# Residual, norm and first projection: squares summed by matmuls, splits and tables made at other times

## The chip, the cores and the metric

The kernel runs on one core of a Trainium2 chip. The metric is the device time of one execution in microseconds (us), the median over several runs. The core's engines run side by side: TensorE (PE, the matmuls; PEld its weight loads), VectorE (DVE), ScalarE (ACT), GpSimd (POOL), and SyncE (SP), which here only issues DMAs. Each engine works through its own list of instructions in order and waits where an operand or a buffer is not ready.

## What is computed

Four layers on x, 512 tokens by 1024 features, in fp32. The first two come from one block, the last two from another. Cut to what matters here:

```python
def first_block(x, c, ...):
    for layer in range(2):
        mod = silu(c) @ w_ada[layer] + b_ada[layer]
        shift, scale, gate = mod[:, :D], mod[:, D:2 * D], mod[:, 2 * D:]
        h = _rms(x, norm_g[layer]) * (1 + scale) + shift
        if layer == 0:
            y = _gdn_mixer(h, ...)            # gated delta rule, ends in @ w_out_a
        else:
            mkv = silu(c) @ w_ada_kv + b_ada_kv
            hk = _rms(x, kv_norm_g) * (1 + mkv[:, D:]) + mkv[:, :D]
            kv = hk @ w_kv                    # keys and values of the attention
            y = _sb_mixer(h, k_sh, v_sh, ...) # stick-breaking attention, ends in @ w_out_b
        x = x + gate * y
    return x

def second_block(x, positions, ...):
    h = rmsnorm(x, norm1_gain)
    # window attention with rope on q and k, mLSTM, both from h @ w_in
    mixed = sigmoid(gate_a) * att_b + sigmoid(gate_m) * ml_b
    x = x + mixed @ w_out
    return x + peer_ffn(rmsnorm(x, norm2_gain), ...)

# rms: x * rsqrt(mean(x * x) + 1e-6) * gain
# stick-breaking: wts = exp(log_sigmoid(logits) + after), after = sum of
# log_sigmoid(-logits) over the keys between this one and the query
```

## The kernel before

Everything lies transposed: x is 8 blocks of 128 features (partitions) by 512 tokens. An fp32 product is three matmuls of a fast fp32 format (`mm3`, L122 to L124) on a high part H, a rounded copy made on ACT (L115), and a low part L, the difference, made on VectorE or POOL (L118). Weights come by DMA as `wr`, are split the same way into `wh` and `wl` by `wtile`, and their low parts go to POOL save for every ninth tile, which goes to VectorE.

**The stages** are gdn (layer 1), the stick-breaking attention (sb, layer 2), a second stage (window attention, mLSTM and `w_out`) and PEER. A scheduler of the framework orders each engine's instructions by a simulated time line. PSUM banks limit it: a projection takes its output bank from `pj`, two of them and now and then one that a stage leaves over.

**The end of a stage** is `residual`: output projection, block j of 8 added to x on VectorE (L346, or L344 without a gate), its square on ACT (L212), a running sum of the squares on VectorE (L214). Behind the last block `mean` sums that one tile over its partitions with `colsum`, four matmuls of 128x128 fp32 against a column of ones (L130), and `rsqrt` makes the reciprocal root: a scale on VectorE (L138), a power on POOL (L139). `rows_of` spreads the four columns by four transposes (L146). `modnorm` then makes each block of the normed x: with a shift a product on VectorE (L234), scale and shift on ACT (L235), the high part on ACT, the low part on VectorE for even blocks and POOL for odd ones; without a shift one instruction on VectorE (L232). The projections of the next stage follow.

A residual can run in parts of its k blocks, each added to x on its own, so that a part can run while later heads are still computed. gdn's takes 7 blocks and 1, sb's

```python
EARLY_A, EARLY_OUT = (slice(0, 7), slice(7, 8)), (slice(0, 6), slice(6, 8))
```

6 and 2; `w_out` has one part.

**sb** goes by 8 pairs of heads (`sb_pair`): logits (L838) with a mask (L841), three ACT operations on them (L846 to L848), a maximum and add on VectorE (L849), the split, the cumulative matmuls (L859), Exp on ACT (L862), the values (L868). Then the product with the gate (L815) and its split into oH and oL, block j of w_out_b's input. While one pair goes through its ACT chain, PE has other pairs' or projections' matmuls.

**The second stage** loads the window masks, the identity and the positions at its start, casts and copies the masks on VectorE (L1204 to L1207) and makes the rope tables from the positions by small VectorE instructions and two sines on ACT (L888 to L906, with a table load for the sine).

## Time and profile before

| what | value |
|---|---|
| median of 3 runs | 2786.94 us (2786.12 to 2788.62) |
| the profiled execution | 2788.73 us |
| its span, first to last instruction | 2786.9 us |
| mean granted clock of TensorE | 0.98 |
| PE busy | 2627.4 us, 94% |
| POOL busy | 1747.1 us, 63% |
| VectorE busy | 1691.1 us, 61% |
| ACT busy | 1207.9 us, 43% |

The three ends of stages lie at 512 to 525 us (gdn to sb), 876 to 901 (sb to the second stage) and 1483 to 1496 (second stage to PEER). In a timeline row the bracket tells how long the engine had been idle before the instruction and which instruction of which engine ended that; a row with xN is N equal instructions in a row, and its us is their whole time.

### The profile page before, as it was taken

The page shows a single profiled execution, that of the slowest core. Times are in us where ns is not written, and L with a number is a line of the kernel's source. Part 1 is how long each engine was busy: PE and PEld are TensorE (multiplying, and loading weights), DVE is VectorE, ACT ScalarE, POOL GpSimd, SP SyncE. Part 2 cuts the span into 40 slices and gives each one's busy share as a digit, 9 for nine tenths or more (in the row PEclk, how much of TensorE's full clock was granted, in tenths as well). Part 3 has the DMA queues.
Part 4 walks back from the last instruction along what each step waited for, and adds up shares of the span by engine and source line. Part 5 has one row for each costly group of instructions (what it writes and reads, how often), then busy time and mean ns, then how long its engine had stood idle before and what let it go on. Part 6 is the DMA issues. An engine that isn't in the chain of part 4 may idle for free. (4 is left out here: it accounts for less than half of the span.)

```text
span 2786.9 us, 40407 instructions
## 1 busy us (share of the span) xinstructions
PE 2627.4 (94%) x14601; PEld 2244.6 (81%) x14601; DVE 1691.1 (61%) x3080; ACT 1207.9 (43%) x2505; POOL 1747.1 (63%) x1350
## 2 busy tenths in 40 slices
PE   6999998799998899999998999999999999999998
PEld 4787777697776787887776889999999977777777
DVE  7767674624445565122232797797875177778886
ACT  5676663635664444233333333434434333333332
POOL 4899883544232533443464378878788478888876
PEclk9999999899998999999999999999999999999999
DMA  6343331222011111211222488888888889999996
GB/s 243 106 139 126 108 109 34 64 92 75 29 35 58 46 52 56 91 63 60 76 83 76 140 293 301 293 309 315 303 302 302 277 306 329 340 331 334 333 315 223
DMA packets 206793, 499.35 MB, mean 179 GB/s; under 512 B 18304, under 2 KB 106624, under 8 KB 203520
## 3 DMA queue, kind: packets, MB, share of 16 engines
q1 hardware_dynamic: 167856, 359.19, 38.2%
q0 software_dynamic: 36864, 134.23, 13.4%
q10 hardware_dynamic: 1872, 3.33, 0.4%
q8 instruction: 115, 1.88, 0.3%
q14 instruction: 86, 0.70, 0.1%
HBM read 444.26 MB, written 52.43 MB: 178 GB/s over the span
## 5 line engine op out<-in xcount | busy, mean ns | idle before, releaser
L118 POOL TENSOR_TENSOR wl<-wr,wh 128x256 fp32r<-128x256 f32 (+2 forms) x515 | 428.8, 852 | 470.6 <-ACT wh L115 431.2
L118 POOL TENSOR_TENSOR upl<-upr,uph 128x1024 fp32r<-128x1024 f32 x128 | 312.2, 2439 | 99.0 <-ACT uph L115 97.8
L115 ACT ACTIVATE wh<-wr 128x256 fp32r<-128x256 f32 (+2 forms) x556 | 228.7, 445 | 323.9 <-PE pj L123 118.4
L122 PE MATMUL pj<-nH,downh 128*128 128x384 f32 x1024 | 352.3, 344 | 2.4 <-ACT w L1567 1.3
L124 PE MATMUL pj<-nH,downl 128*128 128x384 f32 x1024 | 348.8, 341 | 1.8 <-DVE downl L118 1.8
L123 PE MATMUL pj<-nL,downh 128*128 128x384 f32 x1024 | 348.8, 341 | 0.0
L118 POOL TENSOR_TENSOR downl<-downr,downh 128x1024 fp32r<-128x1024 f32 x96 | 238.2, 2483 | 131.9 <-ACT downh L115 130.5
L1612 PE MATMUL acc<-uph,wwh 128*128 128x512 f32 x768 | 302.3, 399 | 9.2 <-ACT wwh L115 9.1
L1612 PE MATMUL acc<-upl,wwh 128*128 128x512 f32 x768 | 305.5, 398 | 0.0
L115 ACT ACTIVATE downh<-downr 128x1024 fp32r<-128x1024 f32 x128 | 135.4, 1059 | 307.8 <-PE pj L123 183.1
L118 DVE TENSOR_TENSOR wwl<-wo,wwh 128x384 fp32r<-128x384 f32 x128 | 205.0, 1603 | 59.1 <-ACT wwh L115 53.7
L1612 PE MATMUL acc<-uph,wwl 128*128 128x512 f32 x768 | 233.1, 399 | 5.5 <-DVE wwl L118 5.4
L122 PE MATMUL pj<-hH,wh 128*128 128x512 f32 x544 | 224.7, 413 | 2.4 <-ACT mo L1284 1.3
L124 PE MATMUL pj<-hH,wl 128*128 128x512 f32 x544 | 221.5, 408 | 0.9 <-POOL wl L118 0.8
L123 PE MATMUL pj<-hL,wh 128*128 128x512 f32 x544 | 215.8, 397 | 0.0
L115 ACT ACTIVATE uph<-upr 128x1024 fp32r<-128x1024 f32 x128 | 134.8, 1053 | 168.5 <-POOL upl L118 114.3
L122 PEld LDWEIGHTS pj<-nH,downh 128*128 128x128 f32 x1024 | 192.9, 188 | 5.4 <-ACT downh L115 1.6
L124 PEld LDWEIGHTS pj<-nH,downl 128*128 128x128 f32 x1024 | 192.9, 188 | 3.0 <-DVE downl L118 2.8
L123 PEld LDWEIGHTS pj<-nL,downh 128*128 128x128 f32 x1024 | 192.9, 188 | 0.3
L1612 PEld LDWEIGHTS acc<-uph,wwh 128*128 128x128 f32 x768 | 145.3, 189 | 48.3 <-ACT wwh L115 13.4
L1612 PEld LDWEIGHTS acc<-uph,wwl 128*128 128x128 f32 x768 | 145.1, 189 | 42.8 <-DVE wwl L118 7.7
L1612 PEld LDWEIGHTS acc<-upl,wwh 128*128 128x128 f32 x768 | 145.4, 189 | 34.9
(627 smaller groups left out, 6546.1 us busy)
## 6 DMA issues: line engine op xcount, KB each, us to landing
downr<-in_peer_down_j SPq DMA_DIRECT2D x128, 512.0 KB
upr<-in_peer_up_j SPq DMA_DIRECT2D x128, 512.0 KB
wr<-in_w_in SPq DMA_DIRECT2D x50, 512.0 KB
ada<-in_w_ada SPq DMA_DIRECT2D x48, 512.0 KB
wait<-w SPq DMA_DIRECT2D x128, 192.0 KB
wo<-wait SPq DMA_DIRECT2D x128, 192.0 KB
G<-stage SPq DMA_DIRECT2D x24, 1024.0 KB
Gt<-G SPq DMA_DIRECT2D x48, 512.0 KB
```

Source lines behind the costliest of these rows:

```text
L115: nc.scalar.activation(h, src, AF.Copy)
L118: return (eb or nc.vector).tensor_tensor(l, src, h.bitcast(F32), op=ALU.subtract)
L122: mm(out, lh, rh, start=start, stop=False)
L123: mm(out, lh, rl, start=False, stop=False)
L124: mm(out, ll, rh, start=False, stop=stop)
L1612: mm(po[z][b], lh[:, zs], rh[:, bs], start=False, stop=j == P - 1 and rh is uh and lh is l, skip_group_check=True)
```

## The change

1. `residual`: the running sum on VectorE is gone. Each block's square goes to a colsum of its own, all eight adding into one PSUM bank ("n", "l" and "q"), and `rsqrt` reads it.
2. w_out_b's parts are 7 blocks and 1.
3. `modnorm` with a shift, even blocks: product with scale and rows in one VectorE instruction, the high part on ACT with the shift as its bias, the low part on VectorE from the same; one ACT instruction less.
4. `wtile` puts the splits of the next weights behind the residual's last square (ACT) and the power (POOL); the splits of the second stage's gate weights stand behind the last normed block.
5. The rope tables are made in `setup`, the window masks in gdn; the identity is cast once. The ones are one column, set by a memset. What sb needs of constants is loaded at its start through a pool of its own.

```diff
-        self.ident, self.ones, sel = self.load_const(const, ("id", "one", "sel"))
+        self.ident, = self.load_const(const, ("id",))
+        self.ones = const.tile([P, 1], F32, name="ones")
+        nc.vector.memset(self.ones, 1.0)
...
+            sel, = self.load_const(tmp, ("sel",))
+            nc.vector.tensor_copy(self.selr, sel[:, :16])
+            self.tables(tmp)
...
+        eb = nc.gpsimd if k % 2 else nc.vector
+        late = late and eb is nc.vector
+        if shift is None or late:
             nc.vector.scalar_tensor_tensor(n, xT[:, k], scale[:, k:k + 1], r, op0=ALU.mult, op1=ALU.mult)
         else:
             nc.vector.tensor_tensor(n, xT[:, k], r, op=ALU.mult)
             nc.scalar.activation(n, n, AF.Identity, scale=scale[:, k:k + 1], bias=shift[:, k:k + 1])
-        self.split(H[:, k], L[:, k], n, eb=nc.gpsimd if k % 2 else nc.vector)
+        if late:
+            nc.scalar.activation(H[:, k], n, AF.Identity, bias=shift[:, k:k + 1])
+            ins = nc.vector.scalar_tensor_tensor(L[:, k], n, shift[:, k:k + 1], H[:, k].bitcast(F32), op0=ALU.add, op1=ALU.subtract)
+        else:
+            ins = self.split(H[:, k], L[:, k], n, eb=eb)
+        if eb is nc.vector:
+            self.normed = ins
...
+        ahead = [self.ahead.pop(0) for _ in range(2)] if self.ahead else []
...
-                for j, raw in enumerate(raws):
-                    self.split(wh[:, j, o], wl[:, j, o], raw[:, fs], eb=nc.gpsimd if self.uid % 9 else nc.vector)
+                with ExitStack() as st:
+                    for ins in ahead:
+                        st.enter_context(self.tc.issue_after(ins))
+                    for j, raw in enumerate(raws):
+                        self.split(wh[:, j, o], wl[:, j, o], raw[:, fs], eb=nc.gpsimd if self.uid % 9 else nc.vector)
...
             if last:
-                held["sq"] = self.square(out, src if scratch is None else scratch(j), held.get("sq"), nc.vector)
+                if j == 0:
+                    held["sums"] = self.pg(bank)
+                sq = src if scratch is None else scratch(j)
+                held["sq"] = nc.scalar.activation(sq, out, AF.Square)
+                self.colsum(held["sums"], sq, 1, j == 0, j == KC - 1)
...
-        self.rms = self.mean([held["sq"]], f"x{self.uid}")
+        self.rms = self.rsqrt(self.const, held["sums"][:, :NT], [NT], 1.0 / D, f"x{self.uid}")
+        self.ahead = [held["sq"].ins, self.power.ins] * 6
...
-    EARLY_A, EARLY_OUT = (slice(0, 7), slice(7, 8)), (slice(0, 6), slice(6, 8))
+    EARLY_A, EARLY_OUT = (slice(0, 7), slice(7, 8)), (slice(0, 7), slice(7, 8))
...
+            self.window_masks(rt)
...
-            idr, sbm, nui = self.load_const(kv, ("id", "sbm", "nui"), F32R)
...
-                idr, wp, wc = self.load_const(c1, ("id", "wp", "wc"), F32R)
...
-                cos, sin = self.rope_tables(c1)
+                idr, wmask, cos, sin = self.identr, self.wmask, self.cos, self.sin
...
+            self.psum(st, q=1)
+            self.residual(a["w_out"], (xH, xL), None, lambda j: x[:, j], x, "q", lambda j: mix[:, j])
```

The line numbers of the changed kernel are higher: L130, L138, L139, L146 and L118 stay, L346 is L367, L838 and L841 are L867 and L870, L859 is L888, L868 is L897.

**First place: PE behind pair 6's logits.** The last logits (`q_6`) and mask of pair 6, then w_out_b's matmuls (into `pj`, from oH and oL). Before; 41 more of these matmuls follow before the first L859 of pair 6:

```order
L838 MATMUL l_7879<-q_6_7787,kT 128x512
L841 MATMUL l_7879<-cr_sbm,cr_id 128x128
L122 MATMUL pj_8158<-oH_6144,wh_8177 128x512
L122 MATMUL pj_8190<-oH_6144,wh_8177 128x512
L123 MATMUL pj_8158<-oL_6145,wh_8177 128x512
L124 MATMUL pj_8158<-oH_6144,wl_8178 128x512
L123 MATMUL pj_8190<-oL_6145,wh_8177 128x512
L124 MATMUL pj_8190<-oH_6144,wl_8178 128x512
L122 MATMUL pj_8214<-oH_6144,wh_8215 128x512
L123 MATMUL pj_8214<-oL_6145,wh_8215 128x512
L124 MATMUL pj_8214<-oH_6144,wl_8216 128x512
L122 MATMUL pj_8214<-oH_6144,wh_8215 128x512
```

After (L888 is the cumulative matmul, on the split `sHb` and `sLb` of pair 6):

```order
L867 MATMUL l_7931<-q_6_7839,kT 128x512
L870 MATMUL l_7931<-cr_sbm,identr 128x128
L122 MATMUL pj_8210<-oH_6196,wh_8229 128x512
L122 MATMUL pj_8245<-oH_6196,wh_8229 128x512
L123 MATMUL pj_8210<-oL_6197,wh_8229 128x512
L124 MATMUL pj_8210<-oH_6196,wl_8230 128x512
L123 MATMUL pj_8245<-oL_6197,wh_8229 128x512
L124 MATMUL pj_8245<-oH_6196,wl_8230 128x512
L888 MATMUL l_7926<-sHb_b_6_7953,cr_nui 128x384
L888 MATMUL l_7926<-sLb_b_6_7954,cr_nui 128x384
L888 MATMUL l_7927<-sHb_b_6_7962,cr_nui 128x384
L888 MATMUL l_7930<-sHa_a_6_7989,cr_nui 128x512
```

Six of w_out_b's matmuls stay ahead of the first cumulative matmul; the others stand behind pair 7's logits.

**Second place: PE at the end of gdn.** The last matmuls of w_out_a, the colsum of the squares `xi`, the transposes of the reciprocal root `rv_x`. Before:

```order
L122 MATMUL pj_4941<-oH,wh_4942 128x512
L123 MATMUL pj_4941<-oL,wh_4942 128x512
L124 MATMUL pj_4941<-oH,wl_4943 128x512
L122 MATMUL pj_4954<-oH,wh_4955 128x512
L123 MATMUL pj_4954<-oL,wh_4955 128x512
L124 MATMUL pj_4954<-oH,wl_4956 128x512
L130 MATMUL pj_4965<-c_one,xi_4858 128x1 x4
L146 MATMUL l_5018<-c_id,rv_x_4970 128x128 x4
```

After, four colsums being further ahead, two behind the fourth of the last eight blocks and two behind the sixth:

```order
L130 MATMUL n_4912<-ones,xi_4725 128x1 x4
L122 MATMUL pj_5000<-oH,wh_5001 128x512
L123 MATMUL pj_5000<-oL,wh_5001 128x512
L124 MATMUL pj_5000<-oH,wl_5002 128x512
L122 MATMUL pj_5016<-oH,wh_5017 128x512
L123 MATMUL pj_5016<-oL,wh_5017 128x512
L124 MATMUL pj_5016<-oH,wl_5018 128x512
L130 MATMUL n_4912<-ones,xi_4768 128x1 x4
L130 MATMUL n_4912<-ones,xi_4811 128x1 x4
L130 MATMUL n_4912<-ones,xi_4854 128x1 x4
L130 MATMUL n_4912<-ones,xi_4897 128x1 x4
L146 MATMUL l_5078<-c_id,rv_x_5030 128x128 x4
```

In place of one colsum behind all blocks four stand there, and four between the blocks.

**Third place: POOL there.** The low parts `wl` of the last w_out_a tile and of sb's first weights (128x512), the power on `rv_x`, the low parts `kL` of odd blocks. Before:

```order
L118 TENSOR_TENSOR wl_4956<-wr_0_4952,wh_4955 128x128
L118 TENSOR_TENSOR wl_5118<-wr_0_5112,wh_5117 128x512
L118 TENSOR_TENSOR wl_5136<-wr_0_5112,wh_5135 128x512
L118 TENSOR_TENSOR wl_5118<-wr_1_5114,wh_5117 128x512
L118 TENSOR_TENSOR wl_5136<-wr_1_5114,wh_5135 128x512
L139 TENSOR_TENSOR rv_x_4970<-rv_x_4970,mhalf 128x4
L118 TENSOR_TENSOR kL<-n_lk_5035,kH 128x512
L118 TENSOR_TENSOR kL<-n_lk_5045,kH 128x512
```

After:

```order
L118 TENSOR_TENSOR wl_5018<-wr_0_5014,wh_5017 128x128
L139 TENSOR_TENSOR rv_x_5030<-rv_x_5030,mhalf 128x4
L118 TENSOR_TENSOR wl_5170<-wr_0_5164,wh_5169 128x512
L118 TENSOR_TENSOR wl_5170<-wr_1_5166,wh_5169 128x512
L118 TENSOR_TENSOR wl_5188<-wr_0_5164,wh_5187 128x512
L118 TENSOR_TENSOR wl_5188<-wr_1_5166,wh_5187 128x512
L118 TENSOR_TENSOR kL<-n_lk_5094,kH 128x512
L118 TENSOR_TENSOR kL<-n_lk_5103,kH 128x512
```

The power moved ahead of the four splits of sb's first weights; those now stand between it and `kL`.

## Rows read from the trace of the kernel before

**Rows 1.** The page, part 1: busy us (share of the span) x instructions.

```profile
PE 2627.4 (94%) x14601; PEld 2244.6 (81%) x14601; DVE 1691.1 (61%) x3080; ACT 1207.9 (43%) x2505; POOL 1747.1 (63%) x1350
```

**Rows 2.** Timeline of ACT: start us, us, engine, line, operation, xcount, [idle before <- releaser].

```profile
10.79 3.75 ACT L212 ACTIVATE sq_l<-x 128x512 f32<-128x512 f32 x7 [0.48 <-DMA x<-in_xT]
...
912.69 0.36 ACT L906 ACTIVATE rope<-rope 128x32 f32<-128x32 f32 x2 [2.09 <-DVE rope L905]
```

**Rows 3.** Stretches: us; busy (x) of PE, PEld, DVE, ACT, POOL; PEclk; DMA share; GB/s.

```profile
512.01:525.00 12.99, 3.03 (x14) 2.55 (x13) 8.94 (x20) 7.92 (x13) 7.33 (x5) 0.64 0.54 178
824.06:836.30 12.24, 11.86 (x51) 9.39 (x51) 8.67 (x14) 10.19 (x23) 6.08 (x6) 1.00 0.01 1
876.04:888.20 12.16, 11.96 (x42) 8.60 (x42) 9.23 (x15) 4.92 (x9) 1.43 (x2) 0.86 0.25 88
888.20:901.00 12.80, 3.08 (x14) 2.58 (x13) 8.22 (x21) 5.38 (x16) 3.84 (x5) 0.61 0.35 111
525.00:530.00 5.00, 4.91 (x23) 4.42 (x23) 3.93 (x6) 5.00 (x9) 2.57 (x2) 0.57 0.00 0
```

**Rows 4.** Timeline of PE at the end of gdn.

```profile
517.08 1.86 PE L130 MATMUL pj<-c_one,xi 128*128 128x1 f32 x8 [5.07 <-DVE xi L214]
520.92 1.11 PE L146 MATMUL l<-c_id,rv_x 128*128 128x128 f32 x4 [1.98 <-POOL rv_x L139]
524.95 0.58 PE L122 MATMUL pj<-wh,kH 128*128 128x256 f32 x1 [2.91 <-ACT kH L115]
```

**Rows 5.** Timeline of ACT there.

```profile
515.45 0.61 ACT L212 ACTIVATE xi<-x 128x512 f32<-128x512 f32 x1
516.08 1.28 ACT L779 ACT_TABLE_LOAD   x1
517.37 0.63 ACT L115 ACTIVATE wh<-wr 128x512 fp32r<-128x512 f32 x1
```

**Rows 6.** Timeline of POOL there.

```profile
513.54 6.36 POOL L118 TENSOR_TENSOR wl<-wr,wh 128x512 fp32r<-128x512 f32 x4 [4.21 <-ACT wh L115]
519.86 1.00 POOL L139 TENSOR_TENSOR rv_x<-rv_x,mhalf 128x4 f32<-128x4 f32 x1
```

**Rows 7.** Timeline of VectorE (DVE) there.

```profile
512.11 0.67 DVE L214 TENSOR_TENSOR xi<-xi,xi 128x512 f32<-128x512 f32 x1
512.71 0.73 DVE L346 SCALAR_TENSOR_TENSOR x<-pj,mods,xi 128x512 f32<-128x512 f32 x1
```

**Rows 8.** Timeline of PE in gdn, a colsum among other matmuls.

```profile
82.79 0.95 PE L130 MATMUL n<-c_one,sq 128*128 128x1 f32 x8
83.60 0.48 PE L122 MATMUL pj<-hH,wh 128*128 128x512 f32 x1
```

**Rows 9.** Timeline of PE at the end of the stick-breaking attention.

```profile
876.04 0.74 PE L122 MATMUL pj<-oH,wh 128*128 128x512 f32 x2 [1.44 <-ACT oH L115]
...
892.95 1.86 PE L130 MATMUL pj<-c_one,sqx 128*128 128x1 f32 x8 [4.73 <-DVE sqx L214]
```

**Rows 10.** Timeline of ACT in pair 6's chain.

```profile
826.96 1.19 ACT L115 ACTIVATE wh<-wr 128x512 fp32r<-128x512 f32 x2
...
830.70 0.65 ACT L115 ACTIVATE sHb_b<-sp_b 128x512 fp32r<-128x512 f32 x1
```

**Rows 11.** Timeline of PE, start of the second stage.

```profile
900.92 0.58 PE L122 MATMUL pj<-wh,hH 128*128 128x256 f32 x1 [3.65 <-ACT hH L115]
...
903.69 0.58 PE L124 MATMUL pj<-wh,hL 128*128 128x256 f32 x1 [1.55 <-DVE hL L118]
```

**Rows 12.** Timeline of VectorE there.

```profile
897.71 0.23 DVE L106 CAST cr_id<-c_id 128x128 fp32r<-128x128 f32 x1 [2.56 <-DMA c_id<-in_consts]
```

**Rows 13.** Timeline of PE at the end of w_out.

```profile
1485.70 1.05 PE L130 MATMUL pj<-c_one,mix 128*128 128x1 f32 x8 [2.17 <-DVE mix L214]
1491.69 1.12 PE L146 MATMUL s<-c_id,rv_x 128*128 128x128 f32 x4 [4.93 <-POOL rv_x L139]
```

**Rows 14.** Timeline of POOL there.

```profile
1490.62 1.01 POOL L139 TENSOR_TENSOR rv_x<-rv_x,mhalf 128x4 f32<-128x4 f32 x1
```

More of the change, by code (lines that the diff above doesn't have):

```diff
@@ L58, in __init__ @@
         self.uid = 0
-        self.rms, self.spare = None, []
+        self.rms, self.spare, self.ahead = None, [], []
         self.wstack = ExitStack()
@@ L138, in rsqrt @@
         nc.vector.tensor_scalar(v, src, scale, EPS, op0=ALU.mult, op1=ALU.add)
[L139 removed]
+        self.power = nc.gpsimd.tensor_tensor(v, v, self.mhalf[:, :n], op=ALU.pow)
         return v
@@ L333, in proj_small, with residual @@
         cb(p[:, :NT * 16].rearrange("p (i c) -> p i c", i=NT))
-    def residual(self, w, act, gate, x_in, x_out, scratch=None, parts=(slice(0, KC),)):
+    def residual(self, w, act, gate, x_in, x_out, bank, scratch=None, parts=(slice(0, KC),)):
         nc = self.nc
@@ L560, in __getitem__ @@
                     return x1[0][at]
-            self.residual(a["w_out_a"], (oH, oL), self.mod0[:, 16:24], x_in, Out(), parts=self.EARLY_A)
+            self.residual(a["w_out_a"], (oH, oL), self.mod0[:, 16:24], x_in, Out(), "n", parts=self.EARLY_A)
             x1 = x1[0]
@@ L816, in sb @@
                     self.split(oH[:, j], oL[:, j], z[j])
-            self.residual(a["w_out_b"], (oH, oL), self.mod1[:, 16:24], lambda j: x1[:, j], x1,
+            self.residual(a["w_out_b"], (oH, oL), self.mod1[:, 16:24], lambda j: x1[:, j], x1, "l",
                           lambda j: wk.tile([P, T], F32, tag="nsq", name=f"sqx2_{j}", bufs=3), self.EARLY_OUT)
@@ L879, with tables, window_masks, rope_tables @@
     GM = 0, 0, 0, 8
-    def rope_tables(self, pool):
+    def tables(self, tmp):
+        self.cos, self.sin = self.rope_tables(self.const, tmp)
+    def window_masks(self, tmp):
+        nc = self.nc
+        wmask = self.const.tile([P, 3, P], F32R, name="wmask")
+        raw = tmp.tile([P, 3, P], F32, name="wmask0")
+        nc.vector.memset(raw[:, 1], NEG)
+        for i, n in ((0, "wp"), (2, "wc")):
+            nc.sync.dma_start(raw[:, i], self.a["consts"][CONST[n]])
+        nc.vector.tensor_copy(wmask, raw)
+        self.wmask = wmask[:, 1:], wmask[:, 0::2]
+    def rope_tables(self, keep, pool):
         nc = self.nc
@@ L1019, in gate_rows @@
         nc.sync.dma_start(w16[0], a["w16_in"])
-        self.split(w16[1], w16[2], w16[0])
+        with self.tc.issue_after(self.normed.ins):
+            self.split(w16[1], w16[2], w16[0])
         p = self.pg()
```

34 lines of the change are left out of this document (15 added, 19 removed).

## The prediction

> **What bounds the kernel now.** I read the busy shares first, then the waits of TensorE (PE) at the ends of stages, then, for each wait, the engine that ended it. PE is busy for 94% of the span [rows 1], so what it does not do are short stretches, and the change touches four of them and the start. At each end of a stage the same chain runs alone: last residual add, square, running sum, colsum (the 4 matmuls against ones), the power on POOL, four transposes, the first block of the norm, the first projection. The stretch tables show it: between 512.01 and 525.00 PE works for 3.03 of 12.99 us at a granted clock of 0.64, and between 888.20 and 901.00 3.08 of 12.80 us at 0.61 [rows 3]. The opposite holds while pair 6 of the stick-breaking attention works through its ACT chain: from the end of its logits at 824.06 to 836.30 PE has 51 matmuls and is busy for 11.86 of 12.24 us at full clock [rows 3]. Those 51 are w_out_b's, and they are what hides that chain. So the question is what the seams give back and what the other split of w_out_b takes.
>
> All sums are made against the profiled execution, 2788.73 us (span 2786.9 and 1.83 around it), which lies 1.79 us above the median of 2786.94; a difference found there is put on the median. The 0.2% that can be told from no change is 5.6 us.
>
> **Start: +1.2 us (0 to +2.5).** ACT now loads the sine table and makes two tables before seven squares. Those squares waited 0.48 us, until 10.79, for x [rows 2]; ACT was free at 10.31. The load takes 1.28 us [rows 5], the two tables took 0.36 where they stand now [rows 2], so the squares start near 11.95, 1.2 us later. VectorE and POOL add these squares and nothing else covers them, so all of it stays on the path; the small VectorE instructions ahead of them have ended by then, since they need positions alone. If something behind is later anyway (adaLN's weights), it is 0.
> At seam 1 the load ends at 517.36 and ACT's next instruction starts at 517.37 [rows 5], so a load costs its 1.28 us there and nothing behind it. The Trainium skill (ScalarE: Activation LUTs, What ACT_TABLE_LOAD costs) adds a drain of about 1380 ns to a load of 1283 ns for each switch; the load agrees, the drain is not in this trace. By the page the start would be +2.6 us.
>
> **Seam 1 (gdn to attention): -4 us (-5 to -2).** Before: colsum ends at 518.94, after PE waited 5.07 us for the running sum [rows 4]. ACT had put splits of the next weights ahead of the last squares, so that the last one ran at 515.45 to 516.06 [rows 5], though its block was ready at 513.44 [rows 7]. After: VectorE loses the 0.67 us add per block [rows 7] and ACT the splits. PE gets the colsums: one put into a warm stream takes from 82.79 to 83.60, 0.8 us and, back to back, 0.95 [rows 8]. Four of them stand between the blocks and four behind (order, second place). Without the adds the last eight blocks lose about 2.6 us (they ran at the pace of add plus gate, 1.40, against 0.7 to 0.75), and gain 3.8 for four colsums: the last block ends at 513.2 in place of 512.01. Three colsums (2.85) then run while the last gate (0.73) and square (0.61) do; the eighth ends near 517.0, 2.0 us earlier. POOL had four splits, 6.36 us, ahead of the power, which so ran at 519.86 to 520.86 [rows 6]; with the power ahead of them (third place) the 1.98 us that PE waited [rows 4] become about 1.1. The first sb matmul then waited 2.91 us [rows 4]; with one ACT operation less on an even block about 1.8. Sum: -2.0 -0.9 -1.1 = -4. What is queued behind: the four splits now run after the power and the odd blocks' low parts behind them on POOL, 6.4 us later than the power; they are wanted some 5 to 9 us after the first matmul, so up to 2 us may come back.
>
> **End of attention and w_out_b: +6.9 us (+3.4 to +10.6).** This term decides. With parts of 7 and 1 in place of 6 and 2, both PSUM banks hold groups that need oH of pair 6 already, so behind pair 6's logits only 6 of the 51 matmuls remain ahead of the first cumulative matmul (first place); the others move behind pair 7's logits and values. Before, from 824.06 to the end of the colsum at 894.81 [rows 9]: 70.75 us. Off goes idle time, 1.44 and 4.73 [rows 9], the slow colsum 1.86, and 1.0 because 48 matmuls between 876.04 and 888.20 took 12.16 us at a clock of 0.86 where 48 x 11.86/51 is 11.16 [rows 3]. That leaves 61.7 us of work. After: 61.7 + 8 x 0.95 = 69.3. To this comes idle time. Six matmuls end at 825.5. The first operand of the cumulative matmuls was made at 830.70 to 831.35, behind a pair of weight splits at 826.96 [rows 10], about 1 us, that now run elsewhere: 830.3. So PE idles 4.8 us, for which I see no cover. Then the low parts come from VectorE about 1.5 us slower than PE takes them, and I allow 1.0 for pair 7, whose first operand is early but whose six leading matmuls wait for oH of pair 6. After such idle time the clock is low for a while: 1.0, as in the 0.86 row. Together 77.6, so +6.9. The lower bound has only the 4.8; the upper one 10 of idle and 2 of clock. The old waits of 1.44 and 4.73 are gone in it, the first because 70 matmuls of the first part now cover pair 7's product, the second because three colsums run while the last square does.
>
> **Seam 2: -3.3 us from the end of the colsum (-5 to -1).** Between the transposes and the first projection at 900.92 lay 3.65 us [rows 11]: VectorE waited 2.56 us for a constant's DMA and then cast masks [rows 12]. All of this is made early now, so the first block follows the rows at once: the product 0.73 as at seam 1 [rows 7], the high part like a square 0.61 [rows 5], with their starts about 1.45 us, so -2.2. The next wait, 1.55 for a low part [rows 11], stood behind the rope's VectorE work; perhaps 1.5 to 2 of it and its successors go. Against that, four of the weight splits now stand ahead of the variance on VectorE, +0.8 after the colsum.
>
> **Seam 3: +1.5 us (-1 to +3.5).** w_out keeps PE full to the end, so six colsums between its blocks lengthen it by 6 x 0.9 = 5.5. Back come the last add with its wait (2.17 us before the colsum, now covered by a seventh colsum), and most of the 4.93 us before the transposes [rows 13], in which the power waited until 1490.62 for POOL's splits [rows 14], 3.9 us after the colsum. The weights' low parts, now behind the power, can be up to 2 late.
>
> **Sum:** 1.2 - 4 + 6.9 - 3.3 + 1.5 = +2.3: 2789.2 us. All else keeps its order.
>
> **Rivals.**
> *Slower by the missing cover.* The 7:1 split costs more: if PE's idle time in pairs 6 and 7 reaches 10 us and the cumulative matmuls run at the low clock behind it, that term is +10.6; with the rest near its middle, +6 to +12, around 2796. It decides from about 8 us of idle time between 825 and 850. For it: only 6 of 51 matmuls stay, and the seams show clocks of 0.61 to 0.64 after such waits. Against: the ACT chain is shorter by the splits that left it.
> *Faster by short seams.* If waits fall below what drops the clock, the projections behind seams 1 and 2 start at full clock. From 525 to 530 PE is busy for 4.91 us at a clock of 0.57 [rows 3], so full clock would give 0.43 x 4.91 = 2.1 us a seam; with the attention's end at +3.4 and the seams at their better bounds the sum is -6 to -11, around 2779. Against: 3 us or more of wait stay in each seam.
> *PE pays for every colsum.* 21 more of them at 0.95 and no gain from the other edits would be +20: 2807. The Trainium skill (Perfetto Trace Analysis, Identifying the Most-Contended Engine) says to improve the engine with the highest occupancy first, and this change moves work from VectorE to it. By that rule the kernel gets slower. The 5.07 and 4.73 us of waiting ahead of two colsums [rows 4, 9] speak against this; seam 3 alone fits.
> That the edits do nothing (the waits kept, the colsums hidden) falls inside the forecast.
>
> **How the numbers follow.** Forecast 0.50, missing cover 0.30, short seams 0.15, every colsum paid 0.05. Of the forecast all lies within 5.6 us of no change; the second and fourth are slower, the third faster. The range leaves out the 0.05 and the outer tails of the second and third: 2778 to 2798.
>
> **What would show it.** Right: PE idle 4 to 6 us ahead of the first cumulative matmul of pair 6; the last colsum of w_out_b 3 to 10 us later against pair 6's logits than the 70.75; first matmuls 1.5 us after the transposes at seam 2; no wait for POOL's power above 1.5 us at seams 1 and 3. Wrong: pair 6's chain ends within 2 us of the fill (then faster), or new waits in the projections behind seams 1 and 3 for POOL's low parts (then slower).

## The result, and the profile after

The changed kernel takes 2818.68 us (median of 4 runs, 2802.48 to 2821.52) against 2786.53 us of the kernel before (4 runs, 2783.68 to 2788.62). The medians lie 32 us apart; the ratio on record is 1.0094, with a 95% interval of 1.0070 to 1.0119: slower by about 26 us (20 to 33), where +2 was forecast and 2798 was the upper end of the range. The profiled run took 2816.81 us (span 2815.0, 1.81 around it), 28.1 more than the profiled run of before.

TensorE's idle time (span less busy) fell from 159.5 us [rows 1] to 150.3, and the kernel is slower all the same, because its busy time rose by 37.3: the colsums (L130) are busy for 36.13 us in place of 16.37, and much of the rest is the same matmuls at a low clock or further apart.

Engines of the changed kernel, from the page (busy us, share of the span, instructions):

```profile
PE 2664.7 (95%) x14769; PEld 2277.1 (81%) x14769; DVE 1680.5 (60%) x3062; ACT 1208.0 (43%) x2498; POOL 1743.0 (62%) x1343
```

Where a loss of 1% lies among many stages is found by cutting both traces at the same instructions of PE. The timeline of PE in the changed kernel at these places (start, duration, engine, line, operation, tiles, shape, count, [idle time before it <- what ended it]):

```profile
25.37 1.12 PE L146 MATMUL n<-c_id,rv_l 128*128 128x128 f32 x4 [3.76 <-POOL rv_l L139]
...
523.64 1.11 PE L146 MATMUL l<-c_id,rv_x 128*128 128x128 f32 x4 [1.35 <-POOL rv_x L139]
527.80 0.58 PE L122 MATMUL pj<-wh,kH 128*128 128x256 f32 x1 [3.05 <-ACT kH L246]
551.01 1.12 PE L787 MATMUL l<-c_id,nsq_k 128*128 128x128 f32 x4 [6.40 <-DVE nsq_k L768]
...
836.03 0.33 PE L870 MATMUL l<-cr_sbm,identr 128*128 128x128 f32 x1
842.66 0.69 PE L888 MATMUL l<-sHb_b,cr_nui 128*128 128x384 f32 x1 [4.85 <-ACT sHb_b L115]
912.22 3.75 PE L130 MATMUL l<-ones,sqx 128*128 128x1 f32 x24
917.41 1.11 PE L146 MATMUL l<-c_id,rv_x 128*128 128x128 f32 x4 [1.45 <-POOL rv_x L139]
920.03 0.58 PE L122 MATMUL pj<-wh,hH 128*128 128x256 f32 x1 [1.50 <-ACT hH L115]
941.89 0.66 PE L787 MATMUL l<-c_id,nsq_ak 128*128 128x128 f32 x2 [3.92 <-POOL rv_ak L139]
...
1520.83 0.72 PE L146 MATMUL s<-c_id,rv_x 128*128 128x128 f32 x4 [1.42 <-POOL rv_x L139]
1575.21 0.44 PE L122 MATMUL pj<-nH,downh 128*128 128x384 f32 x1 [0.77 <-ACT downh L115]
```

The rows of before that answer to them, as far as they did not stand in the rows ahead of the prediction:

```profile
23.98 1.11 PE L146 MATMUL n<-c_id,rv_l 128*128 128x128 f32 x4 [3.75 <-POOL rv_l L139]
...
543.31 1.11 PE L760 MATMUL l<-c_id,nsq_k 128*128 128x128 f32 x4 [2.46 <-DVE nsq_k L741]
823.73 0.33 PE L841 MATMUL l<-cr_sbm,cr_id 128*128 128x128 f32 x1
896.15 1.11 PE L146 MATMUL l<-c_id,rv_x 128*128 128x128 f32 x4 [1.34 <-POOL rv_x L139]
922.23 0.66 PE L760 MATMUL l<-c_id,nsq_ak 128*128 128x128 f32 x2 [3.96 <-POOL rv_ak L139]
```

Differences between such starts give this table (us, before and after; w_out_a starts at 397.04 and 402.82, its last part starts at 502.89 and 507.02, the first logits at 648.68 and 660.39, w_out at 1439.42 and 1466.64, the first down projection at 1544.82 and 1575.21, the last matmul at 2780.37 and 2809.36):

| stretch | before | after | difference | foretold |
|---|---|---|---|---|
| start to the first transposes | 23.98 | 25.37 | +1.4 | +1.2 |
| gdn, to w_out_a's first matmul | 373.1 | 377.5 | +4.4 | 0 |
| to w_out_a's last part | 105.9 | 104.2 | -1.7 | 0 |
| to seam 1's transposes | 18.0 | 16.6 | -1.4 | -2.9 |
| to the first projection | 4.0 | 4.2 | +0.1 | -1.1 |
| to nsq_k's transposes | 18.4 | 23.2 | +4.9 | 0 to +2 |
| to the first logits | 105.4 | 109.4 | +4.0 | 0 |
| to pair 6's last mask matmul | 175.1 | 175.6 | +0.6 | 0 |
| to seam 2's transposes | 72.4 | 81.4 | +9.0 | +6.9 |
| to ak's transposes | 26.1 | 24.5 | -1.6 | -3.3 |
| second stage, to w_out | 517.2 | 524.8 | +7.6 | 0 |
| w_out and seam 3, to the first down | 105.4 | 108.6 | +3.2 | +1.5 |
| PEER, to the last matmul | 1235.6 | 1234.2 | -1.4 | 0 |

The differences add up to +29.0; behind the last matmul the changed kernel ends 0.9 us sooner, which gives the 28.1. Three kinds of loss stand in it: the end of attention, seam 1, and 13.5 us in stretches that the forecast had at nothing.

### The profile page after: what moved, and what is told of

Its sections match the earlier page's. It is cut to its first block, busy times and chain, and to the rows that moved or that the text cites. A ratio compares the mean times of both kernels' runs of the same rounds, so it can differ in the third digit from the quotient of the medians.

```text
span 2815.0 us, 40704 instructions
## 1 busy us (share of the span) xinstructions
PE 2664.7 (95%) x14769; PEld 2277.1 (81%) x14769; DVE 1680.5 (60%) x3062; ACT 1208.0 (43%) x2498; POOL 1743.0 (62%) x1343
## 5 line engine op out<-in xcount | busy, mean ns | idle before, releaser
L118 POOL TENSOR_TENSOR wl<-wr,wh 128x256 fp32r<-128x256 f32 (+2 forms) x508 | 418.7, 843 | 480.2 <-ACT wh L115 449.4
L115 ACT ACTIVATE wh<-wr 128x256 fp32r<-128x256 f32 (+3 forms) x556 | 228.6, 444 | 335.9 <-PE pj L123 141.3
L118 POOL TENSOR_TENSOR upl<-upr,uph 128x1024 fp32r<-128x1024 f32 x128 | 312.4, 2440 | 94.1 <-ACT uph L115 93.4
L118 POOL TENSOR_TENSOR downl<-downr,downh 128x1024 fp32r<-128x1024 f32 x96 | 239.1, 2492 | 132.3 <-ACT downh L115 131.4
L118 DVE TENSOR_TENSOR wwl<-wo,wwh 128x384 fp32r<-128x384 f32 x128 | 207.0, 1620 | 57.9 <-ACT wwh L115 55.8
L1650 PEld LDWEIGHTS acc<-uph,wwh 128*128 128x128 f32 x768 | 145.2, 189 | 48.1 <-ACT wwh L115 14.4
```

Source lines behind the costliest of these rows:

```text
L115: nc.scalar.activation(h, src, AF.Copy)
L118: return (eb or nc.vector).tensor_tensor(l, src, h.bitcast(F32), op=ALU.subtract)
L1650: mm(po[z][b], lh[:, zs], rh[:, bs], start=False, stop=j == P - 1 and rh is uh and lh is l, skip_group_check=True)
```

## The experiments

Times of one kernel on one chip spread widely (the kernel before from 2783.5 to 2801.4 us in one batch), so a ratio settles only what is larger than its interval, 0.3 to 0.6% from end to end. Every ratio below is against the kernel before, with that interval in brackets. What a part does locally is read from the stretches of one profiled run each. The short ones repeat to some tenths of a us; gdn and PEER do not (372.1 to 390.6 and 1228.5 to 1241.0 us over all traces), so a few us there belong to no edit.

**The place of the tiles.** The change's new constants move all later tiles by 1312 bytes a partition: the norm's high parts hH from byte 36384 to 37696. The edit only widens an unused part of one constant tile (40, 48, 88 columns for 32, 64, 224 bytes):

```
-        self.mhalf = const.tile([P, 32], F32, name="mhalf")
+        self.mhalf = const.tile([P, 88], F32, name="mhalf")
```

> The kernel before with the same constant tile 32 bytes longer, so that the activations' parts move from 32 to 0 modulo 64; the order is the same. Address theory: each matmul before PEER takes 233 to 234 ns in place of 229.4, and the time rises by 12 to 20 us to 2799 to 2807, with no other edit. Rival, the run or the chip: 2784 to 2789 as before.

> The changed kernel with one constant tile 32 bytes longer, so that every tile behind it lies 32 bytes higher and the high and low parts of activations start at 32 modulo 64 again, as in the kernel before; every engine's order is the same. Address theory: the 3.5 to 4 ns by which each matmul before PEER is slower in the changed kernel (128x512 at 233.3 ns in place of 229.4) come from these addresses; it goes back to 229 to 230 ns, and the time falls by 12 to 20 us to 2797 to 2808. Rival, the run or the chip: the spacing is the same for any layout, and the time stays at 2815 to 2821.

> The changed kernel with that tile 64 bytes longer: all addresses move, but stay 0 modulo 64. Address theory with a period of 64 bytes: spacing 233 ns and 2815 to 2821 us, as the changed kernel. If any move of the addresses counts, or the run, it may be anything between 2797 and 2821.

> The changed kernel with one unused widening of a constant tile (224 bytes a partition), so that the tiles behind it lie 224 bytes higher: the matmuls' moving operand hH at byte 37920 (32 over a multiple of 256, as in the kernel before, 36384) in place of 37696 (64 over). Nothing else changes, neither an instruction nor its order. Theory (the place of the moving operand in its partition sets how fast matmuls follow each other; the changed kernel pays because its new constant tiles moved everything by 1312 bytes): 128x512 matmuls of the first three stages 229 to 230.5 ns apart as before (233.5 in the changed kernel), the stretch from ak's transposes to w_out 517 to 518.5 us (524.8), from nsq_k's transposes to the first logits 105 to 106.5 (109.4); the whole 10 to 14 us below the changed kernel, ratio against before 1.003 to 1.006. Rival (the spacing belongs to the run or the chip): 233 to 234 ns, 524 to 527 us, ratio 1.007 to 1.010.

Measured: b_shift32 1.0016 [1.0001, 1.0030], a_shift32 1.0069 [1.0038, 1.0100], a_shift64 1.0077 [1.0047, 1.0107], a_shift224 1.0059 [1.0036, 1.0082]. The 12 to 20 us expected of a shift did not come, and the period of 64 bytes is refuted by a_shift32. The spacing is read where PE runs through one and the same 215 recorded matmuls of 128x512 without a wait. First and last of them, in the kernel before, in b_shift32, in the changed kernel and in a_shift224:

```profile
1132.52 0.40 PE L123 MATMUL pj<-aL,wh 128*128 128x512 f32 x1
...
1181.52 0.40 PE L124 MATMUL pj<-hH,wl 128*128 128x512 f32 x1
```

```profile
1133.24 0.40 PE L123 MATMUL pj<-aL,wh 128*128 128x512 f32 x1
...
1183.17 0.39 PE L124 MATMUL pj<-hH,wl 128*128 128x512 f32 x1
```

```profile
1155.28 0.40 PE L123 MATMUL pj<-aL,wh 128*128 128x512 f32 x1
...
1205.22 0.39 PE L124 MATMUL pj<-hH,wl 128*128 128x512 f32 x1
```

```profile
1148.27 0.40 PE L123 MATMUL pj<-aL,wh 128*128 128x512 f32 x1
...
1197.26 0.40 PE L124 MATMUL pj<-hH,wl 128*128 128x512 f32 x1
```

49.00 us before (229.0 ns apart), 49.93 with 32 bytes more, 49.94 in the changed kernel (233.4), 48.99 with 224 bytes more; a_shift32 has 49.72 (232.3), a_shift64 50.13 (234.2). So the spacing goes with the place and comes back with it; my first reading, after three shifts that all gave 232 to 234, was that it belongs to the run, and it was wrong. All 19 traces of this case agree, versions of either place on one chip among them: 228.9 to 229.0 ns in the nine placed as before, 233.3 to 233.4 in the eight placed as the changed kernel or b_shift32. What in the address decides is not settled: 32 over a multiple of 256 gave 229, 64, 96 and 128 over gave 232 to 234.

The second stage, 524.8 us in the changed kernel, is 520.8 in a_shift224, so 4.0 of its +7.6 go with the place, and 1.4 of the +4.0 ahead of the logits (108.0; 517 to 518.5 and 105 to 106.5 were expected). In b_shift32, which has the kernel before's order and differs in the place alone, the second stage takes 524.4 (+7.2 of the +7.6) and the stretch ahead of the logits 108.2 (+2.9). The second stage takes 517.2 to 522.2 us in the nine traces placed as before and 523.9 to 527.4 in the ten others. PEER's matmuls of 128x384 go the other way, by 0.6 ns each (1236.3 us in a_shift224 against 1234.2). On the whole b_shift32 puts the place at +4.5 us (0.16%), with an interval from 0.3 to 8.4; between the versions of the changed kernel it is inside the spread.

**The split of w_out_b.** One line, back to 6 and 2 in the changed kernel, and to 7 and 1 in the kernel before:

```
-    EARLY_A, EARLY_OUT = (slice(0, 7), slice(7, 8)), (slice(0, 7), slice(7, 8))
+    EARLY_A, EARLY_OUT = (slice(0, 7), slice(7, 8)), (slice(0, 6), slice(6, 8))
```

> The changed kernel with the parts of w_out_b back at 6 and 2 blocks, all else as changed. My theory of the prediction: the idle time ahead of the cumulative matmuls of pair 6 (4.8 us in the changed kernel's trace) is gone, and the end of the attention, up to the transposes 9.8 us longer than before, gives back 4 to 8 us: 2810 to 2814. Rival: the colsums and the last part carry that loss, and the split changes less than 2 us.

> The kernel before with one edit: w_out_b in parts of 7 and 1 heads in place of 6 and 2; running sums, norms and tables stay as before. Theory (the split alone is the largest loss: it takes the matmuls away that cover pair 6's ACT chain, and the clock drops behind the idle time): from pair 6's last mask matmul to the transposes of seam 2 the time goes from 72 us to 79 to 82, with one PE wait of 4 to 6 us for sHb_b and about 5 us lost to a low clock around it; the whole +8 to +12 us, ratio 1.003 to 1.0045. Rival (the split costs only together with the colsums between the blocks, which push the last part): 74 to 76 us, +2 to +4, ratio about 1.001.

Measured: a_parts62 1.0025 [1.0006, 1.0043], on the chip where the shifted versions of the changed kernel with 7 and 1 gave 1.0069 and 1.0077; b_parts71 1.0035 [1.0016, 1.0054]. From pair 6's last mask matmul to seam 2's transposes b_parts71 takes 84.3 us (72.4 before), a_parts62 72.7. A row of b_parts71's PE timeline and two of its windows (from:to, length, PE busy (matmuls), granted clock, DMA share, GB/s):

```profile
830.29 0.69 PE L859 MATMUL l<-sHb_b,cr_nui 128*128 128x384 f32 x1 [4.85 <-ACT sHb_b L115]
```

```profile
824.00:830.29 6.29, 1.44 (x6) 0.93 0.00 0
830.29:839.00 8.71, 8.58 (x33) 0.50 0.01 2
```

The split alone makes the wait of 4.85 us and, behind it, 8.7 us of cumulative matmuls at the low clock. All six profiled versions with parts of 7 and 1 have this wait, 4.84 to 4.86 us, and no version with 6 and 2. It is the largest single loss of the change, 8.7 us in the changed kernel (81.4 against 72.7) and 11.9 in the kernel before, and the rival (a cheap split without the colsums) falls.

**Seam 1: norm and sums.** First the old form of the even blocks, then the old running sums on VectorE, both with parts of 6 and 2:

```
-            self.modnorm_block(pool, xT, r, scale, shift, H, L, name, k, tag, bufs, shift is not None)
+            self.modnorm_block(pool, xT, r, scale, shift, H, L, name, k, tag, bufs, False)
```

```
-                held["sq"] = nc.scalar.activation(sq, out, AF.Square)
-                self.colsum(held["sums"], sq, 1, j == 0, j == KC - 1)
+                held["sq"] = self.square(out, src if scratch is None else scratch(j), held.get("sq"), nc.vector)
...
-        self.rms = self.rsqrt(self.const, held["sums"][:, :NT], [NT], 1.0 / D, f"x{self.uid}")
-        self.ahead = [held["sq"].ins, self.power.ins] * 6
+        self.rms = self.mean([held["sq"]], f"x{self.uid}")
```

> The changed kernel with parts of 6 and 2 and the old form of the norm's even blocks (VectorE product, ACT scale and shift, ACT high part, VectorE low part as difference); everything else as changed. Theory (the new form of the even blocks delays the head norm of k: it puts low parts ahead of rv_k on VectorE and one more low part ahead of its power on POOL): PE's wait for nsq_k falls from 6.4 us to 2 to 3.5, the stretch from seam 1's transposes to nsq_k's from 27.4 to 23 to 24.5; the whole 3 to 4 us under the 6:2 version of the changed kernel, ratio against before about 1.001. Rival (POOL's four weight splits, now behind the power, are what delays it): the wait stays at 5 us or more and the ratio at 1.0025.

> The changed kernel with parts of 6 and 2 and the old sum of squares (running sum on VectorE, one colsum at the end, no splits tied behind it) at all three seams; everything else as changed. Theory (per-block colsums shorten seams 1 and 2 by about 2 us each and lengthen w_out by about 1.5): last part of w_out_a to the transposes 18 us (15.6 with the colsums), w_out to the transposes of seam 3 52.5 (54.2); the whole 0 to 4 us above the 6:2 version of the changed kernel, ratio 1.0025 to 1.004. Rival (PE pays for every colsum, 21 x 0.9): 8 us or more below it, ratio under 1.000.

The changed kernel's chain to nsq_k, on ACT, VectorE and POOL:

```profile
542.35 0.58 ACT L763 ACTIVATE nsq_k<-pj 128x512 f32<-128x512 f32 x1
544.42 0.68 DVE L765 TENSOR_REDUCE nss_k<-nsq_k 128x8 f32<-128x512 f32 x1
...
545.77 1.75 POOL L118 TENSOR_TENSOR hL<-n_l,hH 128x512 fp32r<-128x512 f32 x1 [1.95 <-ACT hH L115]
546.28 1.27 DVE L138 TENSOR_SCALAR rv_k<-nss_k 128x8 f32<-128x8 f32 x1
547.62 2.61 POOL L139 TENSOR_TENSOR rv_k<-rv_k,mhalf 128x8 f32<-128x8 f32 x1
550.27 0.69 DVE L768 TENSOR_TENSOR nsq_k<-pj,rv_k 128x512 f32<-128x512 f32 x1 [0.73 <-POOL rv_k L139]
```

The same with the old blocks (a62_oldblock), where the square starts at 543.94, and one row from pair 5:

```profile
545.93 0.16 DVE L138 TENSOR_SCALAR rv_k<-nss_k 128x8 f32<-128x8 f32 x1
546.17 1.64 POOL L139 TENSOR_TENSOR rv_k<-rv_k,mhalf 128x8 f32<-128x8 f32 x1 [0.76 <-DVE rv_k L138]
548.95 0.68 PE L787 MATMUL l<-c_id,nsq_k 128*128 128x128 f32 x4 [2.28 <-DVE nsq_k L768]
...
818.80 0.69 PE L888 MATMUL l<-sHb_b,cr_nui 128*128 128x384 f32 x1 [7.10 <-ACT sHb_b L115]
```

From the start of the square to that of the product it is 7.9 us with the new blocks, 4.3 with the old: the variance stands behind two more norm operations on VectorE and takes 1.27 in place of 0.16, and its power stands behind one more low part on POOL. PE's wait falls from 6.40 to 2.28, and the stretch from seam 1's transposes to nsq_k's from 27.4 to 24.3, as the theory said. The total did not follow (1.0076 [1.0050, 1.0103], in place of 1.001): the planner's order in the pairs changed with it, and PE now waits 7.10 us ahead of a pair's cumulative matmuls. The same wait stands in a62_mended (7.11), consts_only (6.83), consts_late (6.58) and b_nostall (7.11), described below, and in no other version. From the first logits to pair 6's last mask matmul PE goes through 990 recorded matmuls in every trace; these five take them in much the same other order, all others in that of the kernel before but for a few. The stretch takes 181.5 to 185.0 us in the five, 172.4 to 178.4 in the others. b_nostall has no edit in the attention at all, so which order the planner finds there hangs on edits elsewhere.

a62_dvesums (1.0034 [1.0018, 1.0051]) refutes the gain of the colsums, for which 18 us were expected at seam 1 with the sums on VectorE. Its end of w_out_a, and below it that of a_parts62:

```profile
522.60 1.05 PE L130 MATMUL pj<-ones,xi 128*128 128x1 f32 x8 [2.89 <-DVE xi L221]
524.99 1.11 PE L146 MATMUL l<-c_id,rv_x 128*128 128x128 f32 x4 [1.34 <-POOL rv_x L139]
```

```profile
514.72 4.05 PE L130 MATMUL n<-ones,xi 128*128 128x1 f32 x32
520.12 1.11 PE L146 MATMUL l<-c_id,rv_x 128*128 128x128 f32 x4 [1.35 <-POOL rv_x L139]
```

The last parts start at 510.59 and 504.50: 14.4 us to the transposes with the sums on VectorE, 15.6 with the colsums. At w_out it is 53.2 against 54.2, at w_out_b 25.0 against 24.7 from the last cumulative matmul. So over the three ends the colsums lose 1.9 us with parts of 6 and 2. What shortens seam 1, as the two orders read, is that the splits of the next weights stand behind the norm's statistics, which both versions have: no split holds up the last squares on ACT (PE waits 2.89 for the sum, 5.07 before [rows 4]), none holds up the power on POOL (1.34 for 1.98). The tie written for it is not needed: without it the splits stand there too, in consts_only as well.

**Start and gdn.** The tables behind the first adaLN blocks, again with parts of 6 and 2:

```
-            self.tables(tmp)
...
             self.window_masks(rt)
+            self.tables(rt)
```

> The changed kernel with parts of 6 and 2 and the rope tables made behind the first adaLN blocks in place of at the start (the masks and the identity stay early). Theory (the sine table's load in front of the squares and the reload of the exponent's table cost about 2 us at the start): first transposes back by 0.5 us, the wait for v at 61 to 65 us gone, the whole 1 to 2.5 us below the 6:2 version of the changed kernel. Rival (the two table loads of 1.28 us hold ACT up in the adaLN stretch as much as before): no difference or up to 2 us longer.

Measured: 1.0034 [1.0016, 1.0052], no better than a_parts62; the first transposes came at 23.77 (25.05), but gdn took 390.6 us, 359.47 of them busy at a granted clock of 0.96 (346.95 at 0.99 before; 1998 recorded matmuls and 1997). Its trace, like most of this family, shows one VectorE instruction that stands still. In a62_dvesums, on VectorE and POOL, and PE behind it:

```profile
149.53 9.91 DVE L629 TENSOR_SCALAR cols<-rv_q 128x4 f32<-128x4 f32 x1
```

```profile
148.96 2.38 POOL L199 TENSOR_TENSOR ada<-ada,c_rep 128x1024 f32<-128x1024 f32 x1
...
158.69 0.71 POOL L118 TENSOR_TENSOR wl<-wr,wh 128x256 fp32r<-128x256 f32 x1
```

```profile
160.68 1.97 PE L679 MATMUL v<-c_id,Xv 128*128 128x128 f32 x8 [5.49 <-DVE Xv L691]
```

Four numbers a partition take 9.91 us (0.16 to 1.34 in this trace's other heads) and end with the last of eight POOL instructions in a row, at 159.40. In all nine traces in which this instruction takes 6.9 us or more it ends 0.02 to 0.04 us behind the end of a POOL instruction. The first head's product with its inverse (`v<-Xv,kw` on PE, called the end of head 1 here) then starts 148 to 150 us behind the first transposes, else 139.5 to 141 (146 in b_parts71). I folded the instruction away:

```
-        r = self.rsqrt(hd, p[:, :NT], [NT], 1.0, f"q{h}", bufs=2)
-        nc.vector.tensor_scalar(rq, r, DH_SCALE, None, op0=ALU.mult)
+        r = hd.tile([P, NT], F32, tag=f"rv{NT}", name=f"rv_q{h}", bufs=2)
+        nc.vector.tensor_scalar(r, p[:, :NT], DH_SCALE ** -2, EPS, op0=ALU.mult, op1=ALU.add)
+        nc.gpsimd.tensor_tensor(rq, r, self.mhalf[:, :NT], op=ALU.pow)
```

> The kernel before with one small instruction per gdn head left out on VectorE: the query's scale (a 128x4 tensor_scalar, cols<-rv_q) is folded into the sum's scale, so that POOL's power writes cols itself. Theory (that instruction stands still while POOL runs without a gap; in the traces of the kernel before's layout it took 1.1 to 2.0 us in head 1, so it costs that kernel little): ratio against before 0.998 to 1.000, gdn 371 to 376 us. Rival (no effect on either): 0.9985 to 1.0015.

> The changed kernel with the same edit. Theory (in 7 of 10 traces of the changed kernel and its versions this instruction took 6.9 to 9.9 us in head 1, and PE waited 5.5 to 11 us for what stands behind it): gdn from the first transposes to the first matmul of w_out_a 371 to 376 us with no wait for Xv above 2.5 us; the whole 5 to 8 us below the changed kernel, ratio 1.004 to 1.007. Rival (the stall moves to the next such instruction, or was only in the profiled runs): ratio 1.007 to 1.010.

> The changed kernel with w_out_b in parts of 6 and 2 and the same edit. Theory: gdn 371 to 376 us, ratio 0.999 to 1.002, 5 us or more under the 6:2 version's 1.0025 to 1.0045. Rival (the stall has no part in the difference): 1.0025 or more.

Measured: b_nostall 1.0062 [1.0038, 1.0085], a_nostall 1.0103 [1.0079, 1.0128], a62_nostall 1.0054 [1.0034, 1.0075]. The rival held: gdn took 379.3 to 384.9 us, not 371 to 376; in three of the four versions with the edit the stall moved to the next VectorE instruction (5.70 to 8.71 us), in a62_nostall another one stood still earlier (7.97 at 125.01), and the kernel before got it too. VectorE in b_nostall:

```profile
148.39 8.69 DVE L493 SCALAR_TENSOR_TENSOR y<-th,y 128x512 f32<-128x512 f32 x1 [1.68 <-ACT th L492]
```

All four versions with this edit (the fourth follows below) end head 1 at 148 to 149 us. The edit also reorders heads 6 to 8, and b_nostall has the other order in the pairs, so the ratios are not the stall's price alone.

Then the constants part alone (tables, masks, identity; sums, blocks and split as before, tiles placed as before), and the same with late tables:

> Of the whole change only the constants part: tables, masks and the rounded identity made at the start and early in gdn; running sums on VectorE, the old form of the norm's blocks and parts of 6 and 2 as before; tiles placed as before (32 over a multiple of 256). Theory (this is the part that pays; the loss of the 6:2 versions comes from the colsums, the new blocks and gdn's stall): last part of w_out_a to the transposes 14 to 15.5 us (18.1 before), from the first matmul behind them to nsq_k 18.4 to 19.5 us (18.4 before, 23.2 in the changed kernel), seam 2's transposes to the first matmul 2.2 to 2.7 us (4.8), w_out to the transposes 52.3 to 53.3 us, start 1 us later; the whole ratio 0.9975 to 1.0000. Rival (the later start shifts gdn's phase and VectorE's stall in head 1 eats it): the first head ends 148 to 150 us behind the first transposes and the ratio is 1.000 to 1.003.

> As the last, with the rope tables behind the first adaLN blocks in place of the start. Theory: first transposes and the first adaLN stretch as in the kernel before, so that the start's 1 to 2 us come back: ratio 0.997 to 0.9995. Rival (gdn's phase is shifted anyway): ratio 1.000 to 1.003, the first head at 148 to 150 us.

Measured: 1.0033 [1.0014, 1.0052] and 1.0023 [1.0005, 1.0040]. Locally the theory holds: seam 2's transposes to the first projection 2.6 us (4.8 before), seam 1's end 15.1 and 14.4 (18.0), nsq_k 18.9. The rival holds for the whole: head 1 ends at 150.0 and 148.1, and a pair waits for sHb_b (6.83 and 6.58 us) as in a62_oldblock. A part that shortens the seams by some 5 us loses more through a stall (gdn 381.9 and 382.2 us against 373.1) and an order that nobody wrote (pairs 183.5 and 185.0 against 175.1).

**Put together.** Place, split, old blocks and late loads of sbm and nui, step by step; the last with the folded instruction:

> The same 224 bytes, and w_out_b in parts of 6 and 2. Theory (split and place together are nearly all that the change loses): spacing 229 to 230.5 ns, tail from pair 6's last mask matmul to seam 2's transposes 72 to 73.5 us, ratio against before 0.998 to 1.0005. Rival (place without effect): as the 6:2 version, 1.0025.

> The same 224 bytes, parts of 6 and 2, the old form of the norm's even blocks, and the loads and casts of sbm and nui issued behind the norms. Theory: to the kernel with the first two come seam 1's two losses, PE's wait for nsq_k from 6.4 to about 2.5 us and the wait of the first matmul behind the transposes shorter by about 1.5 us: 4 to 5 us less than with place and split alone, ratio against before 0.9965 to 0.9990. Rival (what seam 1 gives back is lost in the pairs behind it, as the version with the old blocks alone suggested): no better than place and split alone.

> The mended version (place of the tiles as before, 6 and 2, old form of the even blocks, sbm and nui behind the norms) with the same edit: the best that the runs so far let me put together. Theory: what is left against before are the shorter seams 1 and 2 (-5 and -3.5), w_out (+1.5) and the start (+1 to +2): ratio 0.997 to 0.9995. Rival (a loss that is not found yet is left in it): 1.001 or more.

Measured: 1.0045 [1.0027, 1.0062], 1.0042 [1.0024, 1.0060], 1.0030 [1.0011, 1.0049]. None beats the kernel before; place and split are not nearly all of the loss. In a62_shift224 the spacing (228.9 ns) and the tail (73.3 us) came as expected, but gdn took 380.4 us, and the losses at seam 1 stayed (nsq_k 23.2); in a62_mended those are gone (19.3), but gdn took 380.5 and the pairs, in the other order, 183.3.

## Why the prediction was wrong, step by step

Forecast +2.3 us, profiled +28.1. Of the 25.8 between them 13.5 lie in stretches that the sum held at nothing, 7.6 at seam 1, 2.1 at the end of attention, 3.6 at the start, seam 2 and seam 3 (less 0.9 behind the last matmul). All four signs that the prediction named for being right came: 4.85 us of idle time, the colsum 8.9 us later, 1.50 at seam 2, 1.35 and 1.42 ahead of the transposes. They looked only where the change was made, and half of the loss lay elsewhere.

**End of attention: right mechanism, mis-sized clock.** PE idles 4.85 us ahead of pair 6's cumulative matmuls, 4.8 foretold. From the end of pair 6's logits (836.36) to the end of the colsum (915.97) it is 79.6 us against 70.75: +8.9, inside its bounds of +3.4 to +10.6. The windows of the changed kernel show the term that failed:

```profile
836.36:842.66 6.30, 1.45 (x7) 0.95 0.00 0
842.66:852.00 9.34, 9.22 (x34) 0.50 0.00 0
852.00:876.93 24.93, 24.84 (x129) 0.99 0.06 22
```

9.22 us of work behind the idle time ran at 0.50, the lower of the clock's two levels, 1.2 GHz: 4.6 us lost where I allowed 1.0. I took that from a stretch at 0.86 [rows 3], while the rows on the seams, at 0.57 to 0.64 [rows 3], stood in the same group. And I misread that row: it counts 42 matmuls, not 48, which at the pace of the 51 are 9.8 of its 12.16 us, so 2.4 were lost there. The idle terms for pair 7 and the low parts (2.5) did not come (5.3 us of idle time in all), and the eight colsums took 8.4 us in place of 7.6. +3.6, -2.5 and +0.8 make the +1.9 by which the stretch passes +6.9: that the term came near is in part luck, errors that cancel.

**Seam 1: wrong sign, +3.6 for -4.** The colsums gave no gain: the last part reached the transposes 1.4 us earlier, and by a62_dvesums that is the splits' new place on ACT and POOL. From the start of the last part to the end of the colsum it is 15.27 us against 16.05: 0.8 less, not 2.0. Before, the blocks ran 1.26 us apart on VectorE (adds to x at 510.19, 511.45, 512.71), not the 1.40 of the sum; after, PE with its colsums takes 3.19 for two (511.32, 514.51, 517.70), 1.6 each. The first projection waited 3.05 in place of 1.8, because VectorE was held by the masks' casts. They took 0.82 and 1.30 us, with POOL at its four splits from 523.56 on, behind the earlier power; before they took 0.23 each, with POOL's splits over. That the splits slow them is not tested; that the masks cost 1.45 us is: with the old blocks that wait is 4.30 in a62_oldblock, and 2.85 in a62_mended, where the masks come behind the norms.

```profile
524.09 0.82 DVE L106 CAST cr_sbm<-c_sbm 128x128 fp32r<-128x128 f32 x1 [1.23 <-DMA c_sbm<-in_consts]
524.83 1.30 DVE L106 CAST cr_nui<-c_nui 128x128 fp32r<-128x128 f32 x1
526.25 0.75 DVE L241 SCALAR_TENSOR_TENSOR n_lk<-x,sck,l 128x512 f32<-128x512 f32 x1
```

And "up to 2 us may come back" was +4.9. I looked for it in POOL's splits; a62_oldblock shows that it comes from the new blocks, ahead of the variance of k and its power: that row of the table falls from 23.2 to 18.9. At the first projection the new blocks gain 1.2, so from the transposes on they cost 3.1.

**Seam 2: right, with part of the size.** The first projection follows 2.6 us behind the transposes and waits 1.50 for the high part (1.45 foretold, 3.65 before [rows 11]). From the end of the colsum to ak it is 25.9 against 27.4: -1.5, inside -5 to -1. PE's idle time there fell by 3.2 us, near the 3.3 foretold, but the same 100 recorded matmuls were busy for 17.40 us in place of 15.72, at a granted clock of 0.70 in place of 0.75: the clock, which this term left out, took half of it back.

**Start and seam 3: about right.** +1.4 for +1.2; to it come 0.7 us of a wait for a weight split at 64.16, beside a third table load in gdn that was not foretold (loads at 61.88, 64.91 and 67.47, two before). Seam 3 and w_out +3.2 for +1.5, just inside the upper bound of +3.5, some 0.6 of it the place of the tiles; the power no longer waits (1.42).

**"All else keeps its order": the step that failed.** The term was put at nothing because the edits leave these stretches alone. The order held, the pace did not: +16.0 us in gdn, ahead of the logits and in the second stage (13.5 with the small gains between them). Their windows, before and then after, show that PE waits no longer there; the same number of recorded matmuls is busy for longer:

```profile
23.98:397.04 373.06, 346.95 (x1997) 0.99 0.40 132
543.31:648.68 105.37, 105.14 (x856) 0.99 0.26 90
922.23:1439.42 517.19, 495.74 (x2936) 0.98 0.19 65
```

```profile
25.37:402.82 377.45, 351.87 (x1997) 0.98 0.41 131
551.01:660.39 109.38, 109.38 (x856) 0.98 0.25 83
941.89:1466.64 524.75, 502.97 (x2936) 0.98 0.19 64
```

Ahead of the logits and in the second stage 5.4 us (by a_shift224) to 10.1 (by b_shift32) of the 11.6 go with the tiles' place, with some 2 to 4 coming back in PEER. In gdn the place is not the cause (377.0 us in a_shift224, 372.1 in b_shift32): its busy time rose by 4.9 at a lower granted clock, and its idle time fell by 0.5. Why the clock is lower there is open, and a part varies from run to run: b_parts71, whose gdn is that of the kernel before in order and place, took 376.5 us, and with before's tiles and, in the second stage, its order, b_nostall had 520.9 us there, not 517.2. The two profiles compared have no long stall in head 1, so it explains nothing of their 28 us; whether the changed kernel meets it more often is open. The 128x4 instruction took 6.9 us or more in 9 of the 12 traces of versions of the change that still have it, and 1.1 to 2.0 in the three of the kernel before (of these b_parts71 has a stall of another instruction there). What is left with parts of 6 and 2 (6 to 15 us by the ratios, 21 in a62_oldblock) has some of its places in the traces: gdn takes 375.7 to 390.6 us in the ten such versions of the change (373.1 before), in four of them the pairs take 6 to 10 us longer in the other order, and w_out and seam 3 lose 1 to 5. How much of a ratio each of them makes, over runs that were not profiled, stays open.

**The rivals.** "Slower by the missing cover" was the right one for its stretch, at nearly its price, by the low clock and not by its 8 to 10 us of idle time. "PE pays for every colsum" holds for the busy time of PE (+19.8 us) and as a sign (seam 1, seam 3), not as a loss: some 2 us of 20, since the colsums stand where PE waited before. The rule behind it (the Trainium skill, Perfetto Trace Analysis, Identifying the Most-Contended Engine) came out on the right side, though most of the loss comes from elsewhere.

## What to carry to other kernels

Work that fills an ACT chain is priced with the clock behind the hole that its removal leaves, from the lowest clock that such a hole shows elsewhere in the trace. A form that saves one engine an operation is checked for the next small chain (variance, power) that has to pass through the same queues. And new constants ahead of everything are no free edit: they move tiles, the start, and with it what meets what.

## What the runs showed of the hardware

- The place of the operands in a partition changed how fast matmuls follow each other: 229.0 ns at one place, 232.3 to 234.2 at three others, for the same 215 matmuls; no bank, port or rule is shown for it.
- A VectorE instruction that takes 0.16 us in other heads stood for 9.91 us (11.51 in consts_only) until the last of a row of POOL instructions had ended. The Trainium skill (SBUF — State Buffer, Who interferes with whom) says that VectorE in its two-port modes and GpSimd contend for a shared port pair, that whoever issues first has it for the whole instruction, and that the other fully blocks. The trace agrees as far as the end of the wait goes, 0.04 us behind the end of a POOL instruction; it differs in that the wait outlasted eight POOL instructions, not one.
